# Feed-forward of a hybrid layer: a new block's token splits one product later and behind the emptying of banks; last product, sum and statistics in column halves

## The chip, the cores and the metric

The kernel runs on one core of a Trainium2 chip. The metric is the device time of one execution in microseconds (us), lower is better. Engines are named as in the profile: PE (TensorE, matmuls), PEld (its weight loads), DVE (VectorE), ACT (ScalarE), POOL (GpSimd), SP (SyncE, which here issues DMAs). Each runs its own instructions in their order and waits for the others by semaphores. PSUM, where PE writes its results, is used in banks of 512 float32 columns.

## The reference, cut to what matters

One layer over 2048 prompt tokens and 8 x 16 sample tokens, with D_MODEL = 1024 and D_FF = 2816. The first part (mLSTM heads, sliding-window attention, output projection, layer norm) isn't touched. The change lies in the feed-forward part and the norm behind it:

```python
def conv_ffn(h, conv_prev, w_up, w_conv, b_conv, w_down):
    T = h.shape[1]
    u = h @ w_up
    ext = jnp.concatenate([conv_prev.astype(u.dtype), u], axis=1)
    c = b_conv + sum(ext[:, j:j + T] * w_conv[j] for j in range(CONV_W))
    a, g = jnp.split(c, 2, axis=-1)
    return (jax.nn.silu(g) * a) @ w_down, ext[:, -(CONV_W - 1):]
...
    f, conv_rows = conv_ffn(h, conv_prev, w_up, w_conv, b_conv, w_down)
    y = layer_norm(DEEPNORM_ALPHA * h + f, ln2_g, ln2_b)
```

All values are float32.

## The kernel before

**Tiles and blocks.** The 17 tiles of 128 tokens are taken in three blocks (`FBLOCKS`): tiles 0 to 5, 6 to 11, and 12 to 16, the last with the sample tokens. The up projection goes, for each block b, over 22 pairs j of column groups (128 value columns and the 128 gate columns that belong to them). Each pair is computed by seven products s = 1 to 7 in the manner of Strassen, from sums of weights and sums of tokens. `f_product` (L1889) issues a product: 12 matmuls, whose moving operand has half the block's tokens as its columns, 384 for blocks 0 and 1 and 320 for block 2. Float32 precision comes from splitting each operand into a high part (ACT casts it, L220) and the low rest (DVE subtracts, L221) in `split`: weights into `uw`, tokens into `hh` (high) and `hl` (low), in the down projection tokens into `fu`.

**Order of the products.** PE's order is that in which the code is written. `self.seq` gives the products of pair j as 6, 2, 5, 3, 4, where the next pair's product 1 stands between 5 and 3, and its product 7 between 3 and 4. A pair holds three PSUM banks A, B, C, in the pool `fup` for even j and `dps` for odd j. Products 1 and 2 go to A, 6, 5 and 3 to B, 7 and 4 to C, and they add up in place, so a bank has to be emptied between certain products.

**Emptying banks.** `f_after` (L1899) does that behind each product: after 1 a copy of A to B (ACT L1910); after 6 a copy of B to `u2` (ACT L1925); after 2 A to `u` (ACT L1927); after 5 B to `u4` (ACT L1929), then C + `u4` to `u` (DVE L1930, and L1932 for the sample tokens); after 3 B to `u` (ACT L1934, L1936); after 4 C + `u2` to `u` (DVE L1939), and then the convolution on `cc` (ACT L1943, DVE L1945) and in `f_gate` the gate `th` (ACT L1967, DVE L1968, L1969), which SP stores to `zf`.

**Tokens of the next block.** At the last pair of a block (j = 21), `f_tokens` (L1764) makes a new block's operands step by step: product s of the old block is followed by the cast and subtraction for the new block's product s, and by sums of tokens in place, `t1` to `t4` (DVE, `hraw`, L1773, L1775, L1777, L1779).

**Order of the other engines.** ACT, DVE, POOL and SP get their order from a scheduler that looks at what each instruction needs and how long it takes in a model of its own. `issue_after(ins)` makes the instructions of a code section that go to the engine of `ins` stand behind `ins` on that engine.

**Down projection.** `f_downs` (L2065) does seven products again per block, each in six units of two tiles of its inner dimension. `d_weights` (wraw to `uw`) and `d_tokens` (r, loaded from `zf`, to `fu`) split its operands ahead of time; the first of them are called in `f_ups` at the last pair of the last block. Results are added to `yacc` (DVE L2128), and normed. The last product of the kernel is s = 3 of block 2, column groups p = 2, 1, 0 in that order; `norm_last` (L1576) takes statistics (BN_STATS, aggregation), and writes the tile out.

Of the kernel before, what the change touches and what calls it, by code (L numbers as in the profile page):

```python
# [14 lines left out]
P = 128  # L15
# [31 lines left out]
HT = 2 * P  # L47
# [157 lines left out]
class Prog:  # L205
# [1380 lines left out]
    def stats(self, y, st=None):  # L1586
        nc = self.nc
        V = nc.vector
        half = st is not None
        if not half:  # L1590
            st = self.wp.tile([P, 2, 6], F32, name="lst", tag="lst", bufs=2)
        mv = self.wp.tile([P, 2], F32, name="lmv", tag="lmv", bufs=2)
        s = self.wp.tile([P, 2], F32, name="lsc", tag="lsc", bufs=2)
        for i in range(half, 2):
            V.bn_stats(st[:, i], y[:, i * 512:(i + 1) * 512])
        V.bn_aggr(mv, st)
# [242 lines left out]
    def f_ups(self, n):  # L1839
        nc = self.nc  # L1840
        for _ in range(AHEAD - n):
            self.f_next()

        self.banks = [[pool.tile([P, 512], F32, name=n, tag=n) for _ in range(3)] for pool, n in ((self.fup, "fup"), (self.dps, "dps"))]
        self.f_written(0)
        self.f_tokens(0, 2)
        late = self.o_late()
        nb = len(FBLOCKS)
        nxt = None
        for i, (b, j, s) in enumerate(self.seq):  # L1850
            if s == 6 and j == 6 and b + 1 < nb:
                nxt = self.f_hT(b + 1)
            if i == 4:
                self.f_written(1)
            if (b, j, s) == (nb - 2, NFF // 2, 6):
                hist = self.f3.tile([P, 2, 2, NFF, DB, 2], F32, name="hist", tag="hist", bufs=1)
                self.sconv, self.convs = hist[:, 0], hist[:, 1]
                nc.sync.dma_start(self.sconv, self.a["sconv"].rearrange("p (v j) b r -> p v j b r", v=2))
            self.f_product(b, j, s)
            while self.made < min(i + 1 + (AHEAD if b == 0 else AHEAD + 2), len(self.seq)):  # L1860
                self.f_next()
            self.f_after(b, j, s)
            if i < 4:
                self.f_tokens(0, *((5,), (3,), ("t4",), (4,))[i])
            if j >= 2 and s in (6, 5):
                next(late, None)
            if nxt and s in (6, 5):
                next(nxt, None)
            if b + 1 < nb and j == NFF - 1:
                if s == 1:  # L1870
                    for _ in nxt:
                        pass
                    nxt = None
                self.f_tokens(b + 1, *{1: (1, "t1", "t3"), 7: (7, "t2"), 6: (6,), 2: (2,), 5: (5, "t4"), 3: (3,), 4: (4,)}[s])
            if b == nb - 1 and j == NFF - 3 and s == 6:
                self.d_begin()
            if b == nb - 1 and j == NFF - 1 and s not in (1, 7):
                self.d_weights()
                if s != 4:
                    self.d_tokens()  # L1880
        nc.sync.dma_start(self.a["conv_p"], self.prev.rearrange("p v j r -> p (v j) r"))
        nc.sync.dma_start(self.a["conv_s"], self.convs.rearrange("p v j b r -> p (v j) b r"))

    def f_written(self, i):

# [13 lines left out]
    def f_after(self, b, j, s):  # L1899
# [6 lines left out]
        WP = W - P if has_s else W  # L1906
        n = WP + (DB * (DS + 2) if has_s else 0)
        A, B, C = [x[:, :h] for x in self.banks[j % 2]]
        if s == 1:
            S.copy(B, A)  # L1910
            return
        if s == 7:
            return
# [8 lines left out]
        m = WP - h  # L1922
        dec = lambda z: z[:, m:].rearrange("p (b l) -> p b l", b=DB)
        if s == 6:
            S.copy(u2, B)  # L1925
        elif s == 2:
            S.copy(u[:, 0, 2:2 + h], A)  # L1927
        elif s == 5:
            S.copy(u4, B)  # L1929
            V.tensor_add(u[:, 1, 2 + h:2 + WP], C[:, :m], u4[:, :m])  # L1930
            if has_s:
                V.tensor_add(us[:, 1, :, 2:], dec(C), dec(u4))  # L1932
        elif s == 3:
            S.copy(u[:, 0, 2 + h:2 + WP], B[:, :m])  # L1934
            if has_s:
                S.copy(us[:, 0, :, 2:], dec(B))  # L1936
        if s != 4:
            return
        V.tensor_add(u[:, 1, 2:2 + h], C, u2)  # L1939
# [125 lines left out]
    def f_downs(self):  # L2065
# [22 lines left out]
        nb, nu = len(FBLOCKS), len(DUNITS)  # L2088
        ys, ops = {}, {}
        last_tile = FBLOCKS[-1][0]  # L2090
        st = self.wp.tile([P, 2, 6], F32, name="st", tag="st", bufs=1)

        def product(s, p, units):
            ps = banks[role[s][2 if p == np_ else p]]
            c = slice(p * P, p * P + P)
            for u in units:
                wh, wl, fh, fl = ops[u]
                n = len(DUNITS[u])
                for k in range(n):
                    for i, (l, r) in enumerate(((fh, wh), (fh, wl), (fl, wh))):  # L2100
                        mm(ps, l[:, k, c], r[:, k], start=s in (1, 4, 7) and u == 0 and k == 0 and i == 0,  # L2101
                           stop=u == nu - 1 and k == n - 1 and i == 2, skip_group_check=True)
# [37 lines left out]
        for g, (b, s, u) in enumerate(self.dseq):  # L2140
# [52 lines left out]
```

## Time and profile before

| | |
|---|---|
| median of 3 runs | 2309.79 us (2309.2 to 2310.85) |
| the profiled execution | 2309.77 us |
| its span on the core | 2308.0 us |
| mean granted clock of PE | 0.998 |
| PE busy | 2275.2 us (99%), 14425 matmuls |
| DVE busy | 1806.0 us (78%), 3157 instructions |
| ACT busy | 1305.2 us (57%), 2465 instructions |
| POOL busy | 228.0 us (10%) |

The span is the time between the first and the last record on the core. Rows of a timeline give start, duration, engine, line, operation, `written tile <- read tiles`, shape and count; in brackets stand the idle time of that engine ahead of the row and what ended it. In timelines a tile's name is that of the program; `u` also stands for `u2` and `u4`. Line numbers are those of the kernel before. Up to 1249 us the up projection is in block 0, from there to 1577 in block 1, then to 1848 in block 2; the down projection follows.

### The profile page before, as it was taken

What the parts mean: (1) busy time and instruction counts of PE and PEld (TensorE: products, weight loads), DVE (VectorE), ACT (ScalarE), POOL (GpSimd) and SP (SyncE); (2) the same over time, 40 slices, a digit from 0 to 9 for tenths busy, and PEclk for the clock granted to TensorE, in tenths of its full rate; (3) what the DMA queues carried; (4) which work ended last, traced back from release to release, by engine and by line L of the source; (5) the groups of instructions that cost most, each with busy time, mean ns of one, the idle gap of its engine ahead of it and who ended that gap; (6) DMA issues with size and microseconds to landing.
All of it is one profiled execution on the core that took longest, in us unless ns stands there. A gap on an engine that the chain in (4) does not pass through costs nothing.

```text
span 2308.0 us, 39905 instructions
## 1 busy us (share of the span) xinstructions
PE 2275.2 (99%) x14425; PEld 2096.7 (91%) x14425; DVE 1806.0 (78%) x3157; ACT 1305.2 (57%) x2465; POOL 228.0 (10%) x289
## 2 busy tenths in 40 slices
PE   8999999999999999999999999999999999999998
PEld 8999999999877778999999999999999988888887
DVE  8777687786689888987888667778766787796897
ACT  5453466776766565555556455556555544654753
POOL 0001001001122121200002000002000000000100
PEclk9999999999999999999999999999999999999999
DMA  8898998889976667787777899888998786756753
GB/s 276 303 316 288 303 321 313 296 301 330 303 253 220 225 209 254 274 323 281 279 270 258 281 310 322 307 305 269 333 293 261 241 286 224 241 196 224 242 188 110
DMA packets 297365, 624.98 MB, mean 271 GB/s; under 512 B 47052, under 2 KB 140240, under 8 KB 297168
## 3 DMA queue, kind: packets, MB, share of 16 engines
q1 hardware_dynamic: 296304, 619.29, 78.4%
q10 hardware_dynamic: 864, 3.15, 0.4%
q8 instruction: 114, 1.87, 0.3%
q14 instruction: 83, 0.68, 0.1%
HBM read 451.78 MB, written 170.56 MB: 270 GB/s over the span
## 4 chain that ended last, share of the span: by engine, by line
PE 71%; DVE 7%; issue 3%; ACT 2%; DMA 2%; POOL 1%; SPq 0%; DVEq 0%; POOLq 0%; ACTq 0%
PE dps L1897 19%; PE fup L1897 19%; PE dps L2101 6%; PE fht L2101 6%; PE fup L2101 5%; PE dps L750 5%; PE dps L225 2%; PE dps L227 2%; PE dps L226 2%; PE ppo L1386 1%; DVE w L221 1%; PE psc L1337 1%; PE ppt L1380 1%; PE dps L775 1%; DMA txy<-wdn 1%
## 5 line engine op out<-in xcount | busy, mean ns | idle before, releaser
L1897 PE MATMUL dps<-hh,uw 128*128 128x384 f32 (+1 forms) x1848 | 477.4, 327 | 5.3 <-DVE u L1930 2.6
L1897 PE MATMUL fup<-hh,uw 128*128 128x384 f32 (+1 forms) x1848 | 476.4, 326 | 0.0
L1945 DVE SCALAR_TENSOR_TENSOR cc<-u,cw,cc 128x768 f32<-128x768 f32 (+1 forms) x264 | 257.8, 978 | 124.4 <-ACT cc L1943 121.0
L1897 PEld LDWEIGHTS dps<-hh,uw 128*128 128x128 f32 x1848 | 329.2, 188 | 7.6 <-DVE u L1930 3.2
L1897 PEld LDWEIGHTS fup<-hh,uw 128*128 128x128 f32 x1848 | 329.3, 188 | 0.0
L1897 PE MATMUL fup<-hl,uw 128*128 128x384 f32 (+1 forms) x924 | 301.3, 326 | 1.5 <-DVE hl L221 1.5
L1897 PE MATMUL dps<-hl,uw 128*128 128x384 f32 (+1 forms) x924 | 301.0, 326 | 0.0
L750 PE MATMUL dps<-w,oh 128*128 128x256 f32 x1344 | 250.5, 282 | 3.5 <-DMA w<-zws 1.8
L750 PEld LDWEIGHTS dps<-w,oh 128*128 128x128 f32 x1344 | 209.3, 188 | 15.8 <-issue 9.6
L220 ACT CAST uw<-wraw 128x1024 fp32r<-128x1024 f32 x126 | 123.3, 981 | 173.7 <-PE dps L2101 104.2
L221 DVE TENSOR_TENSOR w<-wraw,w 128x1024 fp32r<-128x1024 f32 (+1 forms) x155 | 180.9, 1172 | 47.5 <-ACT w L220 45.4
L220 ACT CAST w<-wraw 128x1024 fp32r<-128x1024 f32 (+1 forms) x155 | 155.3, 1009 | 95.7 <-PE dps L750 44.6
L221 DVE TENSOR_TENSOR uw<-wraw,uw 128x1024 fp32r<-128x1024 f32 x126 | 142.6, 1132 | 64.0 <-ACT uw L220 63.8
L750 PE MATMUL dps<-w,ol 128*128 128x256 f32 x672 | 186.2, 277 | 0.0
L1943 ACT ACTIVATE cc<-u,cw 128x768 f32<-128x768 f32 (+1 forms) x132 | 131.9, 1000 | 94.9 <-DVE u L1939 92.1
L1897 PEld LDWEIGHTS fup<-hl,uw 128*128 128x128 f32 x924 | 173.5, 188 | 2.4 <-DVE hl L221 2.4
L1897 PEld LDWEIGHTS dps<-hl,uw 128*128 128x128 f32 x924 | 173.5, 188 | 0.0
L750 PE MATMUL dps<-oh,w 128*128 128x256 f32 x896 | 167.2, 282 | 4.8 <-ACT zev L808 1.6
L2101 PE MATMUL fup<-uw,fu 128*128 128x512 f32 x726 | 169.0, 389 | 0.0
L2101 PEld LDWEIGHTS fup<-uw,fu 128*128 128x128 f32 x726 | 136.2, 188 | 28.2
L2101 PE MATMUL dps<-uw,fu 128*128 128x512 f32 x660 | 161.0, 389 | 0.1
L750 PEld LDWEIGHTS dps<-oh,w 128*128 128x128 f32 x896 | 139.7, 188 | 11.3 <-issue 4.1
(346 smaller groups left out, 4599.4 us busy)
## 6 DMA issues: line engine op xcount, KB each, us to landing
uw<-zw SPq DMA_DIRECT2D x176, 512.0 KB, 4.9
zw<-uw SPq DMA_DIRECT2D x88, 512.0 KB, 3.0
w<-zws SPq DMA_DIRECT2D x72, 512.0 KB, 6.3
wv<-wup SPq DMA_DIRECT2D x66, 512.0 KB, 5.8
wraw<-wi SPq DMA_DIRECT2D x62, 512.0 KB, 5.2
wraw<-zt SPq DMA_DIRECT2D x60, 512.0 KB, 4.3
wraw<-wdn SPq DMA_DIRECT2D x45, 512.0 KB, 3.8
wraw<-wo SPq DMA_DIRECT2D x40, 512.0 KB, 4.8
```

Source lines behind the costliest of these rows:

```text
L220: nc.scalar.copy(hi, src)
L221: nc.vector.tensor_sub(lo, src, hi.bitcast(F32))
L225: mm(out, ah, bh, start=start, stop=False)
L226: mm(out, ah, bl, start=False, stop=False)
L227: mm(out, al, bh, start=False, stop=stop)
L750: mm(o, l, r, start=s in (1, 7) and c == k == i == 0, stop=k == 3 and i == 2, skip_group_check=True)
L775: mm(o, x, w, start=k == i == 0, stop=k == KD - 1 and i == 2, skip_group_check=True)
L1337: nc.tensor.matmul(ps[kvh][:, j, :nk], q[rs, j0 + j], k[rs, sel], start=i == 0, stop=i == 2)
L1897: mm(ps, l[:, k], r[:, k], start=s in (1, 7) and k == 0 and i == 0, stop=k == 3 and i == 2, skip_group_check=True)
L1943: S.activation(c[:, v], u[:, v, 2:2 + n], AF.Identity, bias=w[3], scale=w[2])
L1945: V.scalar_tensor_tensor(c[:, v], u[:, v, i:i + n], w[i], c[:, v], op0=ALU.mult, op1=ALU.add)
L2101: mm(ps, l[:, k, c], r[:, k], start=s in (1, 4, 7) and u == 0 and k == 0 and i == 0, stop=u == nu - 1 and k == n - 1 and i == 2, skip_grou ...
```

## The change

There are three edits.

1. At the last pair of a block, the step of `f_tokens` that belonged behind product s is put into a list `put` and done after the next product. It is issued within `self.behind()`, which puts every instruction in it behind the instructions that empty the banks of that next product, on the engine of each: `f_after` now collects them in `self.gone`.
2. At the last pair of the last block, `d_weights` and `d_tokens` are issued within `self.behind()` too, at the same product as before.
3. The last product's last column group (p = 0) is done in two halves of 256 columns, 27 matmuls each, both in the one bank that it had. Each half is followed by its own addition (`scalar_tensor_tensor`) and statistics (`bn_stats`), so that the statistics tile has 4 groups in place of 2. The statistics behind product 2 of the same tile are taken in two pieces too. The two halves read the same weights, so PE has 54 matmuls of 256 columns for 27 of 512.

```diff
@@ stats @@
-        for i in range(half, 2):
+        for i in range(half if not half or st.shape[1] == 2 else 2, 2):
             V.bn_stats(st[:, i], y[:, i * 512:(i + 1) * 512])
@@ f_ups @@
-                self.f_tokens(b + 1, *{1: (1, "t1", "t3"), 7: (7, "t2"), 6: (6,), 2: (2,), 5: (5, "t4"), 3: (3,), 4: (4,)}[s])
+                put.append((i, b + 1, {1: (1, "t1", "t3"), 7: (7, "t2"), 6: (6,), 2: (2,), 5: (5, "t4"), 3: (3,), 4: (4,)}[s]))
+            if put and put[0][0] < i:
+                _, to, steps = put.pop(0)
+                with self.behind():
+                    self.f_tokens(to, *steps)
             if b == nb - 1 and j == NFF - 3 and s == 6:
                 self.d_begin()
             if b == nb - 1 and j == NFF - 1 and s not in (1, 7):
-                self.d_weights()
-                if s != 4:
-                    self.d_tokens()
+                with self.behind():
+                    self.d_weights()
+                    if s != 4:
+                        self.d_tokens()
+    def behind(self):
+        es = ExitStack()
+        for i in self.gone:
+            es.enter_context(self.tc.issue_after(i.ins))
+        return es
@@ f_after @@
+        self.gone = []
+        gone = self.gone.append
...
-            S.copy(u4, B)
-            V.tensor_add(u[:, 1, 2 + h:2 + WP], C[:, :m], u4[:, :m])
+            gone(S.copy(u4, B))
+            gone(V.tensor_add(u[:, 1, 2 + h:2 + WP], C[:, :m], u4[:, :m]))
...
@@ f_downs @@
-        st = self.wp.tile([P, 2, 6], F32, name="st", tag="st", bufs=1)
+        st = self.wp.tile([P, 4, 6], F32, name="st", tag="st", bufs=1)
-        def product(s, p, units):
-            ps = banks[role[s][2 if p == np_ else p]]
+        def product(s, p, units, q=slice(0, 512)):
+            ps = banks[role[s][2 if p == np_ else p]][:, q]
...
-                        mm(ps, l[:, k, c], r[:, k], start=s in (1, 4, 7) and u == 0 and k == 0 and i == 0,
+                        mm(ps, l[:, k, c], r[:, k, q], start=s in (1, 4, 7) and u == 0 and k == 0 and i == 0,
...
-                    V.bn_stats(st[:, 0], ys[ta][:, :512])
+                    for i in range(2):
+                        V.bn_stats(st[:, i], ys[ta][:, i * HT:i * HT + HT])
...
-                self.norm_last(ys[t], *ln2, a["y"][t], st if t == last_tile else None)
+                self.norm_last(ys[t], *ln2, a["y"][t], None)
...
-                for p in cols:
+                for p in cols[:-1]:
                     product(s, p, range(1, nu))
                     after(s, p)
                     for _ in pending.pop():
                         pass
+                y = ys[last_tile]
+                for i in range(2):
+                    q = slice(i * HT, i * HT + HT)
+                    product(s, cols[-1], range(1, nu), q)
+                    z = y[:, 512:][:, q]
+                    V.scalar_tensor_tensor(z, z, ALPHA, banks[role[s][cols[-1]]][:, q], op0=ALU.mult, op1=ALU.add)
+                    V.bn_stats(st[:, 2 + i], z)
+                self.norm_last(y, *ln2, a["y"][last_tile], st)
```

The scheduler's order on DVE, ACT and SP changes at the three places where a block ends; PE's is the same but for the last product. In the new file the lines of `f_after` and `f_gate` stand 14 further down (L1930 is L1944, L1939 is L1953, L1945 is L1959), but L1910 is L1924.

DVE at the end of block 0, from the first split of the new block's tokens, before:

```order
L221 TENSOR_TENSOR hl_15202<-hraw,hh_15201 128x1536
L221 TENSOR_TENSOR uw<-wg,uw 128x512
L1773 TENSOR_TENSOR hraw<-hraw 128x4x384
L1945 TENSOR_SCALAR cc<-u,cw,cc 128x768
L1775 TENSOR_TENSOR hraw<-hraw 128x4x384
L1939 TENSOR_TENSOR u<-fup,u_15142 128x384
L1945 TENSOR_SCALAR cc<-u,cw,cc 128x768
L221 TENSOR_TENSOR uw<-wv,uw 128x512
L221 TENSOR_TENSOR hl_15240<-hraw,hh_15239 128x1536
L1945 TENSOR_SCALAR cc<-u,cw,cc 128x768
L1777 TENSOR_TENSOR hraw<-hraw 128x4x384
L1945 TENSOR_SCALAR cc<-u,cw,cc 128x768
```

And now:

```order
L221 TENSOR_TENSOR uw<-wg,uw 128x512
L221 TENSOR_TENSOR hl_15218<-hraw,hh_15217 128x1536
L1959 TENSOR_SCALAR cc<-u,cw,cc 128x768
L1773 TENSOR_TENSOR hraw<-hraw 128x4x384
L1953 TENSOR_TENSOR u<-fup,u_15142 128x384
L1775 TENSOR_TENSOR hraw<-hraw 128x4x384
L1959 TENSOR_SCALAR cc<-u,cw,cc 128x768 x2
L221 TENSOR_TENSOR hl_15264<-hraw,hh_15263 128x1536
L1959 TENSOR_SCALAR cc<-u,cw,cc 128x768
L1777 TENSOR_TENSOR hraw<-hraw 128x4x384
L221 TENSOR_TENSOR uw<-wv,uw 128x512
L1944 TENSOR_TENSOR u<-dps,u_15285 128x384
```

The first `hl` has gone behind the weight split `uw<-wg`, and the add from the bank C (`u<-dps`, L1930, now L1944) has come forward: before, it stood behind two more `hl`, which follow it now.

ACT at the end of block 2, from the copy to `u2` of product 6 (L1925, now L1939) to the copy to `u4` of product 5 (L1929, now L1943), before:

```order
L1925 COPY u_21339<-dps 128x320
L220 COPY fu<-r_21083 128x768
L220 COPY fu<-r_21083 128x384
L1927 COPY u<-dps 128x320
L220 COPY uw<-wraw 128x1024
L1967 ACTIVATE th<-cc 128x656
L1929 COPY u_21340<-dps 128x320
```

And now, from the cast ahead of it:

```order
L220 COPY fu<-r_21083 128x384
L1939 COPY u_21339<-dps 128x320
L220 COPY uw<-wraw 128x1024
L220 COPY fu<-r_21083 128x768
L1981 ACTIVATE th<-cc 128x656
L1941 COPY u<-dps 128x320
L220 COPY uw<-wraw 128x1024
L220 COPY fu<-r_21083 128x768
L1943 COPY u_21340<-dps 128x320
```

Casts for the down projection (`uw<-wraw`, `fu<-r`) that stood ahead of the `u2` copy stand behind it now, so two `uw` and two `fu` of 768 columns lie between the two copies where one `uw` and two `fu` lay.

DVE at the same place, to the add of product 4 (L1939, now L1953), before:

```order
L1968 TENSOR_SCALAR th<-th,cc 128x656
L1930 TENSOR_TENSOR u<-dps,u_21340 128x192
L1969 TENSOR_TENSOR th<-th,cc 128x656
L1932 TENSOR_TENSOR u<-dps,u_21340 128x8x16
L221 TENSOR_TENSOR uw<-wraw,uw 128x1024
L221 TENSOR_TENSOR fu<-r_21083,fu 128x768
L1939 TENSOR_TENSOR u<-dps,u_21339 128x320
```

And now:

```order
L221 TENSOR_TENSOR uw<-wraw,uw 128x1024
L221 TENSOR_TENSOR fu<-r_21083,fu 128x768
L1982 TENSOR_SCALAR th<-th,cc 128x656
L221 TENSOR_TENSOR uw<-wraw,uw 128x1024
L1983 TENSOR_TENSOR th<-th,cc 128x656
L221 TENSOR_TENSOR fu<-r_21083,fu 128x768
L1944 TENSOR_TENSOR u<-dps,u_21340 128x192
L1946 TENSOR_TENSOR u<-dps,u_21340 128x8x16
L221 TENSOR_TENSOR uw<-wraw,uw 128x1024
L221 TENSOR_TENSOR fu<-r_21083,fu 128x768
L221 TENSOR_TENSOR uw<-wraw,uw 128x1024
L221 TENSOR_TENSOR fu<-r_21083,fu 128x768
```

The add of product 4 follows as the next row: two `uw` and two `fu` stand between it and the adds of product 5, where one pair stood.

PE at the kernel's end, with the waits that an instruction carries, now:

```order
L2115 MATMUL dps<-uw,fu 128x512 [waits DVE_49]
L2115 MATMUL dps<-uw,fu 128x512
L2115 MATMUL fht<-uw,fu 128x512 x27
L2115 MATMUL fht<-uw,fu 128x256 x27
L2115 MATMUL fht<-uw,fu 128x256 [waits DVE_49]
L2115 MATMUL fht<-uw,fu 128x256 x26
```

Before, the last column groups were 54 matmuls of 512 columns without a wait among them; now the second half's first matmul waits for an instruction of DVE, which is the first half's addition from the same bank.

More of the change, by code (lines that the diff above doesn't have):

```diff
@@ L1847, in f_ups @@
         late = self.o_late()
-        nb = len(FBLOCKS)
+        nb, put = len(FBLOCKS), []
         nxt = None
@@ L1908, in f_after @@
         A, B, C = [x[:, :h] for x in self.banks[j % 2]]
+        self.gone = []
+        gone = self.gone.append
         if s == 1:
-            S.copy(B, A)
+            gone(S.copy(B, A))
             return
@@ L1924, in f_after @@
         if s == 6:
-            S.copy(u2, B)
+            gone(S.copy(u2, B))
         elif s == 2:
-            S.copy(u[:, 0, 2:2 + h], A)
+            gone(S.copy(u[:, 0, 2:2 + h], A))
         elif s == 5:
-            S.copy(u4, B)
-            V.tensor_add(u[:, 1, 2 + h:2 + WP], C[:, :m], u4[:, :m])
+            gone(S.copy(u4, B))
+            gone(V.tensor_add(u[:, 1, 2 + h:2 + WP], C[:, :m], u4[:, :m]))
             if has_s:
-                V.tensor_add(us[:, 1, :, 2:], dec(C), dec(u4))
+                gone(V.tensor_add(us[:, 1, :, 2:], dec(C), dec(u4)))
         elif s == 3:
-            S.copy(u[:, 0, 2 + h:2 + WP], B[:, :m])
+            gone(S.copy(u[:, 0, 2 + h:2 + WP], B[:, :m]))
             if has_s:
-                S.copy(us[:, 0, :, 2:], dec(B))
+                gone(S.copy(us[:, 0, :, 2:], dec(B)))
         if s != 4:
             return
-        V.tensor_add(u[:, 1, 2:2 + h], C, u2)
+        gone(V.tensor_add(u[:, 1, 2:2 + h], C, u2))
         c = self.f3.tile([P, 2, 768], F32, name="cc", tag="cc", bufs=2)[:, :, :n]
```

## The prediction, made before the changed kernel was run

> **What bounds the kernel now.** I read the page's busy times first: PE is busy 99% of the span of 2308.0 us, so the edits can matter only where PE waits, or after its last product. I went through PE's timeline at the two block changes, at the change to the down projection and at the end, then the chain of waits and the other engines there. PE's stops, in start, duration, engine, line, operation and idle time with its releaser:
>
> ```profile
> 1249.60 0.34 PE L1897 MATMUL fup<-hh,uw 128*128 128x384 f32 x1
> 1250.82 0.44 PE L1897 MATMUL dps<-hh,uw 128*128 128x384 f32 x1 [0.88 <-DVE u L1930]
> ...
> 1575.05 0.31 PE L1897 MATMUL fup<-hh,uw 128*128 128x320 f32 x1
> 1577.08 0.45 PE L1897 MATMUL dps<-hh,uw 128*128 128x384 f32 x1 [1.73 <-DVE u L1930]
> ...
> 1843.12 0.31 PE L1897 MATMUL dps<-hh,uw 128*128 128x320 f32 x1
> 1844.53 0.42 PE L1897 MATMUL dps<-hh,uw 128*128 128x320 f32 x1 [1.10 <-ACT u L1929]
> ```
>
> Records of queued matmuls overlap, so I count from start to start. A 384-column matmul starts 0.17 us after the one before it (6.24 us for 36), a 320-column one 0.15 (5.27 for 36): a product of 12 takes 2.08 or 1.76. PE thus loses 1.05, 1.88 and 1.26 us at these seams; each time product s=4 or 3 wants a bank that DVE or ACT has not emptied. All three seams together hold 4.2 us.
>
> ```profile
> 1548.86 6.24 PE fup L1897 x36
> 1579.43 5.27 PE fup L1897 x36
> ```
>
> **Seam from block 0 to 1.** ACT's and DVE's timelines:
>
> ```profile
> 1231.63 1.48 ACT L220 CAST hh<-hraw 128x1536 fp32r<-128x1536 f32 x1
> 1233.53 0.47 ACT L1934 COPY u<-fup 128x384 f32<-128x384 f32 x1
> ...
> 1233.14 1.76 DVE L221 TENSOR_TENSOR hl<-hraw,hh 128x1536 fp32r<-128x1536 f32 x1 [1.82 <-ACT hh L220]
> 1237.09 1.01 DVE L1945 SCALAR_TENSOR_TENSOR cc<-u,cw,cc 128x768 f32<-128x768 f32 x1
> 1246.88 3.42 DVE L221 TENSOR_TENSOR hl<-hraw,hh 128x1536 fp32r<-128x1536 f32 x2
> 1250.22 0.55 DVE L1930 TENSOR_TENSOR u<-dps,u 128x384 f32<-128x384 f32 x1
> ```
>
> DVE stands idle 1.82 us ahead of the first hl and then never until the add on which PE waits. Queued operations overlap by about 0.08 (two hl in 3.34, where one is 1.75), so a place in this queue costs hl or hraw 1.67, cc 0.93, u 0.47 and uw (0.69 for 512, below) 0.60. After the change the cast of hh sits behind ACT's copy of product 3, so it cannot begin before that copy has run: hh lands about 1233.7 and hl begins about 1235.25 (the copy's own start is PE-bound, about 1233.3, since the cast ahead of it is gone). The uw split of 0.60 that followed hl runs in the gap. DVE therefore has 2.1 - 0.6 = 1.5 us less of its queue done when hl starts. The add L1930 goes forward past several splits, which clears the old stall, but those splits are still due. In the new order DVE has from hl up to the add that empties C for the next column pair's product 4: 7 hl and 4 hraw (11 x 1.67), 8 cc (7.44), 4 u (1.88) and 5 uw (3.0), 30.7 us, all queued. That add starts at 1235.25 + 30.7 - 0.47 = 1265.5, and PE restarts 0.60 after an add's start (1250.82 against 1250.22), at 1266.1. Unstalled, PE wants that bank seven products after 1249.77, at 1264.33. So it loses 1.75 in place of 1.05: **+0.7**. Bounds: 0, if DVE has hidden slack, and +1.5, the lost DVE time in full.
>
> **Seam from block 1 to 2.** The same edit, with 320 columns:
>
> ```profile
> 1559.30 0.48 ACT L1934 COPY u<-fup 128x384 f32<-128x384 f32 x1
> 1558.89 1.49 DVE L221 TENSOR_TENSOR hl<-hraw,hh 128x1280 fp32r<-128x1280 f32 x1 [1.24 <-ACT hh L220]
> 1575.00 0.95 DVE L1969 TENSOR_TENSOR th<-th,cc 128x768 f32<-128x768 f32 x1
> 1576.47 0.55 DVE L1930 TENSOR_TENSOR u<-dps,u 128x384 f32<-128x384 f32 x1
> ```
>
> hl moves from 1558.89 to about 1560.98 (copy to 1559.7, cast 1.27). Up to the add stand 6 hl or hraw at 1.40, 4 cc, u, 2 th (1.8) and 2 uw, 15.6, then the add itself: it ends at 1577.1, where it ended before at 1577.02. Nothing is won here, because the splits that went behind it only paid for the lateness. They now come after it: 4 hl, 1 hraw (7.0), 4 cc (3.7), 3 uw (1.8), and the adds of both products (0.95), 13.5 more, to 1590.6. PE wants that bank after one product of 2.08 and six of 1.76, 12.64 after its restart at 1577.2, at 1589.8. A new stop of 0.8 to 1.05: **+1.0**, bounds 0 and +1.5.
>
> **Seam into the down projection.** ACT first, then DVE:
>
> ```profile
> 1837.55 0.84 ACT L220 CAST fu<-r 128x768 fp32r<-128x768 f32 x1
> 1840.07 0.41 ACT L1925 COPY u<-dps 128x320 f32<-128x320 f32 x1
> 1842.08 1.05 ACT L220 CAST uw<-wraw 128x1024 fp32r<-128x1024 f32 x1
> 1843.41 0.75 ACT L1967 ACTIVATE th<-cc 128x656 f32<-128x656 f32 x1 [0.27 <-DVE cc L1945]
> 1844.07 0.41 ACT L1929 COPY u<-dps 128x320 f32<-128x320 f32 x1
> ...
> 1846.17 1.22 DVE L221 TENSOR_TENSOR uw<-wraw,uw 128x1024 fp32r<-128x1024 f32 x1
> 1847.30 0.95 DVE L221 TENSOR_TENSOR fu<-r,fu 128x768 fp32r<-128x768 f32 x1
> 1848.43 0.49 DVE L1939 TENSOR_TENSOR u<-dps,u 128x320 f32<-128x320 f32 x1 [0.18 <-PE dps L1897]
> 1852.49 0.55 DVE L221 TENSOR_TENSOR fu<-r,fu 128x384 fp32r<-128x384 f32 x1
> 1854.67 0.84 DVE L1968 SCALAR_TENSOR_TENSOR th<-th,cc 128x656 f32<-128x656 f32 x1 [0.82 <-ACT th L1967]
> 1855.43 0.69 DVE L221 TENSOR_TENSOR uw<-wraw,uw 128x512 fp32r<-128x512 f32 x1
> ```
>
> Before, ACT had cast early what it now keeps for later. From the u2 copy (begun 1840.25, after a small fu cast) to the u4 copy it now has uw, fu, th, a u copy, uw and fu between the two copies; at the rows' durations less some 0.1 of overlap 0.96 + 0.73 + 0.66 + 0.32 + 0.96 + 0.73 = 4.36. With 0.32 for the u2 copy and 0.41 for u4 that ends about 1845.35. PE is ready at 1843.27, so it stops 2.1 in place of 1.26: +0.8. Next late is DVE: from the first uw (about 1841.9) it has uw, fu, th, uw, th, fu (1.14 + 0.87 + 0.76 + 1.14 + 0.76 + 0.87) and the two u adds, to about 1848.0, while PE wants bank C at 1845.45 + 1.76 = 1847.2: a second stop, between 0.3 and 0.9, 0.8 by the longer durations that follow a cross-engine wait. Together **+1.55**.
>
> Then the last gate. Behind the second u add DVE has uw, fu, uw, fu (4.0) before it adds product 4, so the add starts at 1851.9 where it started at 1848.43: 3.5 late. The fu after it grows from 384 to 768 columns (+0.4), a uw slips into the idle 0.82 (-0.6). The last th is 3.3 to 3.4 late, of which 1.55 is PE's own delay: 1.75 is new. Who waits: SP stores th to zf, reads it back as r, and DVE, ACT and PE follow. The chain of waits runs through it until PE:
>
> ```profile
> 1857.28 4.09 DMA zf<-th
> ...
> 1895.33 2.79 PE dps L2101 x11
> ```
>
> As this chain had no slack before, the lateness arrives in full at 1895: **+1.75**; bounds 0, if the loads are held by something else, and 2.5, if they queue behind shifted loads.
>
> **Costed at nothing.** SP's loads at the seams move by a place or two; PE's releasers there are DVE and ACT, so the loads have been early, and if one is not, it lies within the bounds above. The statistics of product 2's half in two pieces (one more DVE operation, under 0.5) run under the PE work ahead of the last product. No instruction of POOL changes its place.
>
> **Tail.** PE, DVE, and last a row of 256-column matmuls from earlier in the kernel:
>
> ```profile
> 2288.01 12.40 PE L2101 MATMUL fht<-uw,fu 128*128 128x512 f32 x54
> 2294.33 0.69 DVE L2128 SCALAR_TENSOR_TENSOR yacc<-yacc,fht 128x512 f32<-128x512 f32 x1 [0.72 <-PE fht L2101]
> 2297.41 1.41 DVE L1583 SCALAR_TENSOR_TENSOR yacc<-yacc,lsc,f_ln_b 128x512 f32<-128x512 f32 x2
> 2300.45 0.69 DVE L2128 SCALAR_TENSOR_TENSOR yacc<-yacc,fht 128x512 f32<-128x512 f32 x1 [1.63 <-PE fht L2101]
> 2301.89 0.21 DVE L1596 BATCH_NORM_AGGREGATE lmv<-st 128x2 f32<-128x12 f32 x1
> ...
> 77.14 1.60 PE L759 MATMUL psx<-w,xs 128*128 128x256 f32 x12
> ```
>
> 54 matmuls of 512 come at 0.227; 27 end about 2294.15. A 256-column one is near 0.116 (11 starts in 1.32), so halving costs nothing by itself: the first half is done by 2297.4. Both halves share one bank, and in the new order the second half's first matmul waits on DVE, on the first half's add. That add is queued behind the norm of the tile before, to 2298.75, and takes some 0.42, an estimate along the line from 0.69 for 512 columns and 0.49 for 320. PE restarts at 2299.2, needs 27 x 0.116 = 3.1 to 2302.35, and after it come 0.15 of drain, add and statistics of 256, near 0.45 each: aggregation at 2303.5 in place of 2301.89, **+1.65**. Without the wait it would be PE at 2300.4 and aggregation at 2301.3, -0.55: these are the bounds.
>
> The Trainium skill ("PSUM — Partial Sum Buffer", section "PSUM bank collisions raise a hardware error") says to guard PSUM by bank and quadrant, not by address, since two engines collide at different addresses of one bank too. By that rule the halves of one bank cannot overlap, which is the +1.65; by addresses alone it would be the -0.55. No run here shows a collision.
>
> **Sum.** 0.7 + 1.0 + 1.55 + 1.75 + 1.65 = 6.65. The profiled execution took 2309.77, beside the median of 2309.79, so 2316.5.
>
> **Rivals.** *The seams clear* (other side): PE's three stops of 4.2 go and the tail overlaps (-0.55), 2305.0. It decides if DVE has 2 us of spare time within the 17 us after a block change, or the second half needs no add. For it: the adds on which PE waits do move forward. Against: DVE's only idle there lies ahead of hl, and it grows. 6%. *The lateness is absorbed* at the two block changes and in the down chain, leaving 1.55 + 1.65: 2313.0. For it: DVE later idles again (78% busy); against: PE needs the bank within 15 us. 17%. *The down chain drags more*: the later splits free wraw and r later, and one more transfer like zf<-th, 4.09 from issue to landing, comes to lie on the path for some 2.5 of it: 2319. 9%. *The clock drops* at the tail's stop of 1.7 us, and the last 27 matmuls take twice their 3.1: 2319.6, 2%. Against it stands a stop of 1.88 us, after which this row grants 1.00 (its last three columns are clock, DMA share, GB/s):
>
> ```profile
> 1576.80:1590.00 13.20, 12.92 (x86) 12.92 (x87) 12.92 (x16) 6.94 (x13) 5.56 (x4) 1.00 0.68 221
> ```
>
> The Trainium skill ("TensorE: Matmul & The Clock Gate", section "Part 1: The HAM clock gate") puts the drop after an idle window of about 3.4 us; the trace agrees as far as it goes, with 1.88 us and no drop.
>
> **How the numbers follow.** My forecast has 66%: 2316.5. Its terms' bounds give 2311.5 with the chains slack and 2319 with them long; that takes in the absorbed case and leaves out the cleared seams and the far ends. This kernel's measurement tells about 0.2%, 4.6 us, from no change. Faster: 6%. Same: absorbed 15 and the forecast's low edge 4, 19%. Slower: 62 of the forecast, 11 of the last two, 2 of the absorbed, 75%.
>
> **What would show it.** At both block changes: DVE's idle ahead of the first hl near 3.3 and 2.7 in place of 1.82 and 1.24, no PE stop at block 0's last product 4, one of about 1.5 fifteen microseconds later; two stops of 1.9 and 1.0 after block 1. Into the down projection two stops, 2.1 and 0.8, and the last th 3.3 late against its place before. At the end a hole of some 1.7 us in the middle of the last product's 54 short matmuls. No hole, or PE stops shorter than before, would make it wrong.

## The result, and the profile after

The changed kernel takes 2326.1 us (median of 6 runs, 2324.34 to 2329.03) where the kernel before takes 2310.32 (6 runs, 2309.2 to 2313.08). The ratio is 1.0065, with a 95% interval of 1.0054 to 1.0075: 15 us slower, between 12.5 and 17.3. The forecast was 2316.5, in a range of 2311.5 to 2319. The direction was right; the time lies outside the range, and some 8 to 10 of the 15 us have another cause than any that was named.

The profiled execution has a span of 2324.7 us (2308.0 before) and a granted clock of 0.999. PE's busy time is the first thing to look at. It was 2275.2 us and is now this:

```profile
PE 2292.4 (99%) x14452; PEld 2111.7 (91%) x14452; DVE 1806.3 (78%) x3160; ACT 1305.3 (56%) x2465; POOL 216.1 (9%) x289
```

PE has 27 matmuls more, since 54 of half the width stand for 27, so its work is the same. Yet it is *busy* 17 us longer; stops would show as idle time instead. PE's stops in the timeline after (start, duration, engine, line, operation, idle time with its releaser) are these:

```profile
1260.08 0.44 PE L1909 MATMUL fup<-hl,uw 128*128 128x384 f32 x1 [0.19 <-DVE hl L221]
1273.81 0.44 PE L1909 MATMUL fup<-hh,uw 128*128 128x384 f32 x1 [1.14 <-DVE u L1944]
...
1586.94 0.45 PE L1909 MATMUL dps<-hh,uw 128*128 128x384 f32 x1 [1.80 <-DVE u L1944]
1600.41 0.41 PE L1909 MATMUL fup<-hh,uw 128*128 128x320 f32 x1 [0.52 <-DVE u L1946]
...
1855.82 0.41 PE L1909 MATMUL dps<-hh,uw 128*128 128x320 f32 x1 [1.91 <-ACT u L1943]
1858.38 0.41 PE L1909 MATMUL dps<-hh,uw 128*128 128x320 f32 x1 [0.54 <-DVE u L1946]
...
2314.08 3.49 PE L2115 MATMUL fht<-uw,fu 128*128 128x256 f32 x27 [1.70 <-DVE yacc L2187]
```

They stand where the prediction put them: the old stop at the change to block 1 is gone and one of 1.14 follows 13.7 us later, the other two changes have two stops each, and there is a hole in the middle of the last product. They don't make 15 us.

PE's order is the same in both kernels up to the last product, so the n-th matmul of one trace is that of the other. How late the changed kernel starts the same matmul shows the stages:

```
matmul, and when it starts before            later in the change by   in this stage
 6789,  916 us  start of the up projection        6.1                    6.1
 8700, 1249 us  last pair of block 0              7.7                    1.6
 9000, 1302 us  past the change to block 1        8.6                    0.9
10550, 1568 us  last pair of block 1              9.8                    1.2
10700, 1593 us  past the change to block 2       10.7                    0.9
12380, 1839 us  last pair of block 2             10.5                   -0.2
12470, 1855 us  past the change to down          12.2                    1.7
12643, 1895 us  where the old chain ended        12.5                    0.3
14370, 2288 us  last column groups               14.8                    2.4
the span's end                                   16.7                    1.9
```

Six microseconds are lost before the feed-forward begins, in code that the change doesn't touch and whose instructions stand in the same order. The view of groups by shape shows how (line, engine, operation, count, busy us, mean ns of one, idle time before). First the kernel before, then the change:

```profile
L750 PE MATMUL dps<-w,oh 128*128 128x256 f32 x1344 | 250.5, 282 | 3.5 <-DMA w<-zws 1.8 <-DVE zev L822 0.8 <-ACT zev L808 0.6
L750 PE MATMUL dps<-w,ol 128*128 128x256 f32 x672 | 186.2, 277 | 0.0
L750 PE MATMUL dps<-oh,w 128*128 128x256 f32 x896 | 167.2, 282 | 4.8 <-ACT zev L808 1.6 <-DVE zev L820 1.2 <-ACT oh L544 1.1
L1897 PE MATMUL fup<-hl,uw 128*128 128x384 f32 x616 | 206.1, 335 | 1.5 <-DVE hl L221 1.5
L2101 PE MATMUL fup<-uw,fu 128*128 128x512 f32 x726 | 169.0, 389 | 0.0
L1897 PE MATMUL fup<-hh,uw 128*128 128x320 f32 x616 | 144.4, 309 | 0.0
```

```profile
L750 PE MATMUL dps<-w,oh 128*128 128x256 f32 x1344 | 256.5, 285 | 1.7 <-DMA w<-zws 0.6 <-ACT zev L808 0.6 <-DVE zev L822 0.4
L750 PE MATMUL dps<-w,ol 128*128 128x256 f32 x672 | 188.2, 280 | 0.0
L750 PE MATMUL dps<-oh,w 128*128 128x256 f32 x896 | 171.7, 285 | 4.5 <-ACT zev L808 1.5 <-ACT oh L544 1.2 <-DVE zev L820 0.9
L1909 PE MATMUL fup<-hl,uw 128*128 128x384 f32 x616 | 207.4, 337 | 1.8 <-DVE hl L221 1.8
L2115 PE MATMUL fup<-uw,fu 128*128 128x512 f32 x726 | 170.3, 391 | 0.0
L1909 PE MATMUL fup<-hh,uw 128*128 128x320 f32 x616 | 144.4, 309 | 0.5 <-DVE u L1946 0.5
```

The matmuls of 256 columns from `w` and `oh` or `ol` are 3 ns longer on average, those of 384 and 512 are 2 ns, those of 320 are not. A few nanoseconds are nothing on one instruction, but line L750 has 3360 of them, so 3 ns make some 10 us. Part of that falls into waits that PE had there anyway (in the first row its idle time shrinks from 3.5 to 1.7), and 6 us are left. What the first 900 us share with the change is memory: a tile's place is fixed for the whole program. The statistics tile `st` grew from 2 x 6 to 4 x 6 floats, 48 to 96 bytes per partition, which take 64 and 96 in the compiled program's table of tiles. What is placed behind it lies 32 bytes further, among it `oh`, `ol`, part of `hh` and `hl`, `r`, `u`, `cc`, `yacc`, and two of the ten slots of `uw`. The `w` of L750 and the `fu` stay where they were. The theory for the experiments is that this shift slows the matmuls that read there; its rivals are the placement of the instructions, and the waits.

### The profile page after: what moved, and what is told of

It is laid out like the page before. It is cut to its first block, busy times and chain, and to the rows that moved or that the text cites. A ratio compares the mean times of both kernels' runs of the same rounds, so it can differ in the third digit from the quotient of the medians.

```text
span 2324.7 us, 39954 instructions
## 1 busy us (share of the span) xinstructions
PE 2292.4 (99%) x14452; PEld 2111.7 (91%) x14452; DVE 1806.3 (78%) x3160; ACT 1305.3 (56%) x2465; POOL 216.1 (9%) x289
## 4 chain that ended last, share of the span: by engine, by line
PE 85%; DVE 9%; issue 3%; DMA 2%; ACT 1%; SPq 0%; POOL 0%; DVEq 0%; ACTq 0%; POOLq 0%
PE fup L1909 19%; PE dps L1909 18%; PE dps L750 15%; PE fup L2115 6%; PE dps L2115 6%; PE fht L2115 5%; PE dps L225 2%; PE dps L775 2%; PE dps L227 2%; PE dps L226 1%; PE ppo L1386 1%; PE psc L1337 1%; DVE w L221 1%; DVE uw L221 1%; PE ppt L1380 1%
## 5 line engine op out<-in xcount | busy, mean ns | idle before, releaser
L1959 DVE SCALAR_TENSOR_TENSOR cc<-u,cw,cc 128x768 f32<-128x768 f32 (+1 forms) x264 | 257.6, 978 | 128.8 <-ACT cc L1957 125.6
L750 PE MATMUL dps<-w,oh 128*128 128x256 f32 x1344 | 256.5, 285 | 1.7 <-DMA w<-zws 0.6
L750 PEld LDWEIGHTS dps<-w,oh 128*128 128x128 f32 x1344 | 211.1, 188 | 13.4 <-issue 8.9
L750 PE MATMUL dps<-w,ol 128*128 128x256 f32 x672 | 188.2, 280 | 0.0
L750 PE MATMUL dps<-oh,w 128*128 128x256 f32 x896 | 171.7, 285 | 4.5 <-ACT zev L808 1.5
L750 PEld LDWEIGHTS dps<-oh,w 128*128 128x128 f32 x896 | 141.1, 188 | 11.1 <-issue 4.1
```

The costliest lines, as they stand in the source:

```text
L750: mm(o, l, r, start=s in (1, 7) and c == k == i == 0, stop=k == 3 and i == 2, skip_group_check=True)
L1959: V.scalar_tensor_tensor(c[:, v], u[:, v, i:i + n], w[i], c[:, v], op0=ALU.mult, op1=ALU.add)
```

## The experiments

A lateness is that of PE against the kernel before at the same matmul, in one profile of each. At 916 us kernels that are alike up to there differ from -1.3 to +3.4 us in single profiles (in the two with the most the clock had fallen at 893 us, see the last section), so lateness is read by stage behind that point, and the pace of equal matmuls ahead of it. The medians of the kernel before, taken anew beside each group of runs, lie between 2309.69 and 2310.4.

**The statistics tile alone.** Only the size is changed; no instruction moves.

```diff
-        st = self.wp.tile([P, 2, 6], F32, name="st", tag="st", bufs=1)
+        st = self.wp.tile([P, 4, 6], F32, name="st", tag="st", bufs=1)[:, :2]
```

> The kernel before, with only the statistics tile st made [P, 4, 6] as in the change and two of its four groups used: 96 bytes per partition for 48, every instruction in its old order, tiles allocated behind st (oh, ol, part of hh and hl, r, u, cc, yacc and two of ten uw slots) 32 bytes further. Theory 'addresses' (the pace of matmuls in the changed kernel falls because operands start 32 bytes off a 64-byte boundary): slower by 10 to 12 us, some 2320.5 to 2322, with PE about 6 us late at the start of the up projection and 9 to 9.5 us late at the end of its block 1, and no new stop at a seam. Rival 'instructions' (more and differently placed instructions slow PE): 2310, no difference. Rival 'seams' (all the rest comes from the new waits): 2310.

Measured: 2319.99, ratio 1.0036 (1.0023 to 1.0049), about 8 us slower, just less than was expected. The lateness is 6.0 us at 916 us, 7.5 at the last pair of block 1, where 9 or more was expected, and 10.8 at the last column groups. The changes between blocks have no new stop; there is one of 0.6 in block 2, at 1680.6. The 256-column group has the changed kernel's mean:

```profile
L750 PE MATMUL dps<-w,oh 128*128 128x256 f32 x1344 | 256.5, 285 | 0.9 <-DMA w<-zws 0.7 <-ACT zev L816 0.2
```

The instructions are those of the kernel before in the same order with the same waits, so neither a new instruction nor a new wait did it. The matmuls of `psx<-w,xs` serve as a control: they have 256 columns too, neither of their operands moved, and they keep their pace (117.6 ns from start to start on average, before and here).

**The whole change at the old addresses.** The four statistics groups live in a spacer that the down projection has anyway, and a spacer of 64 bytes holds the place of `st`.

```diff
-        self.skew(self.fp, 480)
+        st = self.fp.tile([P, 120], F32, name="skew", tag="skew480", bufs=1)[:, :24].rearrange("p (i k) -> p i k", k=6)
...
-        st = self.wp.tile([P, 4, 6], F32, name="st", tag="st", bufs=1)
+        self.skew(self.wp, 64)
```

> The changed kernel whole, but with the four statistics groups kept in a spacer of 480 bytes that the down projection has anyway, and a spacer of 64 bytes in the place of st: all tiles at the addresses of the kernel before, all instructions in the order of the change. Theory 'addresses': pace as before, the new stops stay: 0.6 + 0.8 + 1.6 at the seams and 1.7 to 2 at the end, 2310 + 5 = 2314 to 2316. Rivals 'instructions' and 'seams': 2325 to 2327, as the change.

Measured: 2315.71, ratio 1.0022 (1.0013 to 1.0031), 5 us slower, as expected. The two halves, 1.0036 and 1.0022, make 1.0058 together where the change has 1.0065, within their intervals. The lateness at 916 us is -0.5 now, and the 256-column group of `w` and `oh` is back at 283 ns.

**Which way, and how far.** Six more sizes and places. `st` of 120 bytes moves the same tiles by 64:

> The kernel before with the statistics tile of 120 bytes, which takes 128: the same tiles as in the run with 96 bytes now 64 bytes further, not 32. Theory 'addresses' in the form 'off a 64-byte boundary': 2310, no difference. In the form 'any move hurts, since the spacers were chosen for these very addresses': 2315 to 2322. Rivals: 2310.

Measured: 2324.77, ratio 1.0057 (1.0044 to 1.0069): worse than by 32 (its fastest execution is slower than the slowest of that run), and above the 2322 expected. A 64-byte boundary is not the rule. Only the first part's tiles by 32 further, and by 32 nearer (`skew(self.xp, 288)` and `skew(wx, 416)`, then 224 and 480, for 256 and 448):

> The kernel before with the 32 bytes put only under the tiles of the first part (oh, ol and its working tiles), and taken back ahead of the feed-forward's. Theory 'addresses': the share of the first 880 us alone, +5 to +6 us, 2315 to 2316, with matmuls of 256 columns from oh and ol going from 0.114 to 0.117 us, and the feed-forward at its old pace. Rivals: 2310.

> The kernel before with the tiles of the first part 32 bytes nearer to the start, the feed-forward's at their old place. If the pace goes by the distance from the old address in the same direction as the steps seen (0.114 us as before, 0.118 with 32 more, 0.120 with 64 more): 0.111 and 6 us faster in the first 880 us, 2304. If the old address is the best one or the two sides are alike: 0.117 and 2314 to 2316.

Measured: 2314.62, ratio 1.0017 (1.0008 to 1.0027), with 117 to 118 ns from start to start, by the medians, where `oh` and `ol` took 113 to 114, and no lateness added behind 916 us; and 2317.15, ratio 1.0027 (1.0017 to 1.0038), with 117 to 118 ns too. Both sides of the old address are slower, so the hoped-for gain of 6 us isn't there. Only the feed-forward's tiles by 32 (`skew(self.wx, 736)` for 704):

> The kernel before with 32 bytes more only ahead of the feed-forward's tiles; the first part at its old addresses. If the shares add up: nothing up to 915 us, +2 to +3 in the up projection's blocks 0 and 1, next to nothing in block 2 (320 columns), +2.5 to +3 in the down projection, 2314.5 to 2316 in all; the rival that the loss is one thing of the whole program and not of the operands: 2310 or 2320.

Measured: 2315.69, ratio 1.0026 (1.0017 to 1.0036). Behind 916 us the lateness grows by 0.2 in block 0 and the change to block 1, by 1.2 in block 1, not at all in block 2, and by 2.8 in the down projection. By the medians the two shares, 4.2 and 5.4 us, add up to the 9.6 that the shift of all tiles costs (by the ratios, some 4 and 6 where it costs 8, which their intervals allow). Last, all tiles by 128 and by 256:

> The kernel before with st taking 192 bytes for 64: the same tiles 128 bytes further. 32 less, 32 more and 64 more have all been slower. If the pace comes back with a period of 128 bytes: 2310. If the period is longer: 2320 to 2326.

> The same with 320 bytes, tiles 256 bytes further. If the pace comes back with a period of 256 bytes or less: 2310. If the period is 512 or more, or it is no matter of a period: 2318 to 2328.

Measured: 2324.43, ratio 1.0065 (1.0049 to 1.008); and 2308.44, ratio 0.9997 (0.9988 to 1.0006). With 256 bytes the pace is back, in every group:

```profile
L750 PE MATMUL dps<-w,oh 128*128 128x256 f32 x1344 | 250.6, 282 | 2.1 <-DVE zev L822 1.1 <-DMA w<-zws 0.6 <-ACT zev L816 0.3
L2101 PE MATMUL fup<-uw,fu 128*128 128x512 f32 x726 | 169.0, 389 | 0.0
```

In the down projection the moving operand is `uw`, the stationary one `fu`, which never moved. Only two of the ten `uw` slots did, the high and low part of every fifth unit. Start-to-start times there in ns, means of six matmuls in a row, from matmul 13100 on, in the kernel before, in the changed kernel (32 bytes on) and with 256 bytes:

```
before        226.7 226.7 226.7 226.7 226.7 226.7 226.7 226.7 226.7 226.7 226.7 226.7 226.7 226.7 226.7 226.7 226.7 226.7 226.7 226.7 226.7 226.7
32 bytes on   226.7 226.7 226.7 226.7 228.2 233.3 231.7 230.2 226.7 226.7 226.7 226.7 226.7 226.7 226.7 226.7 226.7 226.7 231.7 233.2 233.5 232.0
256 bytes on  226.7 226.7 226.7 226.7 226.7 226.7 226.7 226.7 226.7 226.7 226.7 226.7 226.7 226.7 226.7 226.7 226.7 226.7 226.7 226.7 226.7 226.7
```

One unit in five takes up to 233 ns for 227, as one unit in five has its moving operand in a shifted slot; the others keep their time to a tenth of a nanosecond. So the loss goes with the operand's place, matmul by matmul, and not with a load on the memory as a whole.

**The first edit alone, at the old addresses.** The diff is the part of the change in `f_ups` on `f_tokens`, with `behind` and `gone`.

> The kernel before with the first edit alone (a new block's splits one product later and behind the emptying), all tiles at their old addresses. Theory 'DVE is late by the same work': +0.6 at the change to block 1 and +0.8 to +1.7 at the change to block 2, 2311.5 to 2312.5 in all, with a PE stop about 13 us after each change that was not there; the end as before. Rival 'the edit clears the stops and its loss in the changed kernel came from the slower matmuls': -2.9, 2307.

Measured: 2310.98, ratio 1.0004 (0.9995 to 1.0013), less than expected, and not to be told from no change; the stages can. The change to block 1 costs 0.7, that to block 2 costs 1.7, and the stop of 1.12 after the first is there as in the change:

```profile
1253.01 0.44 PE L1908 MATMUL fup<-hl,uw 128*128 128x384 f32 x1 [0.23 <-DVE hl L221]
1266.74 0.45 PE L1908 MATMUL fup<-hh,uw 128*128 128x384 f32 x1 [1.12 <-DVE u L1943]
...
1578.48 0.44 PE L1908 MATMUL dps<-hh,uw 128*128 128x384 f32 x1 [1.86 <-DVE u L1943]
```

The rival, that the stops clear, falls: without the slower matmuls they cost what they did with them, and at the change to block 2 more. The second stop after block 1 is missing here for another reason, told in the last section.

**One product later, but not behind the emptying.**

```diff
-                with self.behind():
-                    self.f_tokens(to, *steps)
+                self.f_tokens(to, *steps)
```

> The kernel before with the new block's splits one product later, but not put behind the emptying, at the old addresses. Theory 'DVE is late by the idle time ahead of the first hl': the first hl as early as before or near to it, the add that PE waits for ahead of two splits, and the stops at the two block changes shorter than before: -0.5 to -2, 2308 to 2309.5. Rival 'one product later is the loss': +1.3 to +2.5 as with the whole edit.

Measured: 2308.4, ratio 0.9995 (0.9986 to 1.0004). By stage it gains 0.8 at the change to block 1 and 0.6 at that to block 2. The first hl is as early as before, behind the same idle 1.82:

```profile
1231.49 1.76 DVE L221 TENSOR_TENSOR hl<-hraw,hh 128x1536 fp32r<-128x1536 f32 x1 [1.82 <-ACT hh L220]
```

In the change that idle time is 0.99 and 2.25 around one weight split:

```profile
1239.91 0.69 DVE L221 TENSOR_TENSOR uw<-wg,uw 128x512 fp32r<-128x512 f32 x1 [0.99 <-ACT uw L220]
1242.85 1.76 DVE L221 TENSOR_TENSOR hl<-hraw,hh 128x1536 fp32r<-128x1536 f32 x1 [2.25 <-ACT hh L220]
```

So the first edit has a half that gains 1.4 us by the stages, which two medians can't tell from nothing, and a half that loses more: `issue_after` on the copy makes DVE wait.

**The second edit alone, at the old addresses.** `d_weights` and `d_tokens` within `self.behind()`.

> The kernel before with the second edit alone (the down projection's first splits behind the emptying), at the old addresses. Theory: two stops of 2.1 and 0.7 at the change to the down projection in place of one of 1.26, +1.5 to +1.7, and nothing at 1895 us, since the chain from th by zf to r has slack: 2311.5 to 2312. Rival, as the prediction had it: the last th 3.3 late and the chain without slack, +3.3, 2313.

Measured: 2310.37, ratio 1.0004 (0.9995 to 1.0014), again less than expected. The lateness rises by 2.3 at the change to the down projection (0.7 more than in the change itself, for which the last section has a fall of the clock) and by 0.06 from there to matmul 12643 at 1895 us. The prediction's last gate costs nothing.

**The last product's halves in two banks, at the old addresses.** What the old bank held is added ahead of the last two column groups; the halves of the rest start in two banks that are free by then.

```diff
+                add(last_tile, 1, banks[role[s][cols[-1]]], True)
...
-                    product(s, cols[-1], range(1, nu), q)
+                    product(s, cols[-1], range(1, nu), q, banks[i][:, :HT])
-                    V.scalar_tensor_tensor(z, z, ALPHA, banks[role[s][cols[-1]]][:, q], op0=ALU.mult, op1=ALU.add)
+                    V.tensor_add(z, z, banks[i][:, :HT])
```

> The kernel before with the third edit, but with the halves in two banks that are free by then (what the old bank held is added to yacc ahead of the last two column groups), at the old addresses. Theory 'the shared bank costs the end': no hole in the 54 short matmuls, aggregation 0.5 earlier than before against 1.8 later in the change, 2309.5 to 2310 beside 2310. Rival 'the halves themselves cost' (54 short matmuls slower than 27 long ones, or DVE held by the norm of the tile ahead): +0.5 or more.

Measured: 2309.22, ratio 0.9995 (0.9986 to 1.0005). The hole is gone, in PE's and DVE's timelines at the end:

```profile
2295.23 6.63 PE L2101 MATMUL fup<-uw,fu 128*128 128x256 f32 x54
...
2299.85 0.41 DVE L2174 TENSOR_TENSOR yacc<-yacc,fup 128x256 f32<-128x256 f32 x1
2301.90 0.42 DVE L2174 TENSOR_TENSOR yacc<-yacc,fup 128x256 f32<-128x256 f32 x1 [1.18 <-PE fup L2101]
2302.82 0.26 DVE L1596 BATCH_NORM_AGGREGATE lmv<-skew 128x2 f32<-128x24 f32 x1
```

PE is 1.1 us late here by its first part, so aggregation is at 2301.7 in the kernel before's time, for 2301.89: a gain of 0.2, where 0.5 was expected. The 54 short matmuls take 6.63 us from the first start to the last end where 27 long ones took 6.28, and that is the rest. In the change the same rows stand 2 us further apart:

```profile
2313.62 0.41 DVE L2187 SCALAR_TENSOR_TENSOR yacc<-yacc,fht 128x256 f32<-128x256 f32 x1
2317.61 0.42 DVE L2187 SCALAR_TENSOR_TENSOR yacc<-yacc,fht 128x256 f32<-128x256 f32 x1 [3.12 <-PE fht L2115]
2318.52 0.26 DVE L1596 BATCH_NORM_AGGREGATE lmv<-st 128x2 f32<-128x24 f32 x1
```

## Why the prediction was wrong

**The step that failed** is the one under "costed at nothing": the statistics in smaller pieces were counted as one more DVE operation of under 0.5 us, hidden under PE. The tile that holds them was not looked at. Its growth from 48 to 96 bytes moves every tile placed behind it, and that costs 8 us by the run with the tile alone, about 11 of its profile's span, where the whole change has 15 and 16.7. The prediction held each matmul's duration for given and asked only for waits; 3 ns on a 256-column matmul was outside all of its rivals. One other step failed, the last gate below. Where the prediction looked at stops, its signs came: DVE idle for 3.24 us ahead of the first hl (3.3 was named), the pairs of stops, and a hole of 1.70 in the last product.

**The change to block 1**: +0.7 predicted, +0.7 measured in the run with the first edit alone; the change has 0.9, of which the run with the tile alone has 0.1 too. Stops of 0.34 and 1.31, counted from start to start, stand for one of 1.05. The old stop goes, and DVE's lateness comes due 13.7 us later, as the sum over its queue said. Its start held too: hl begins at 1242.85, which is 1235.2 without the lateness of 7.7, where 1235.25 was said. (The 1233.7 at which hh was said to land is where its cast begins.)

**The change to block 2**: +1.0 predicted, +0.9 measured. The stop that stays is 1.97 against 1.88, the new one 0.69.

**The change to the down projection**: +1.55 predicted, +1.6 measured (1.7 less 0.1 of pace), by stops of 2.07 and 0.70 where the prediction had 2.1 and 0.8.

**The last gate**: +1.75 predicted, nothing measured, in the change and in the run with the second edit alone. The last th starts at 1869.68, 13.6 later than before (1856.03), of which 10.5 is PE's lateness up to this seam: 3.1, near the 3.3 predicted. But the step "as this chain had no slack before" was wrong. The trace of before had a row that says so:

```profile
1876.69 0.84 ACT L220 CAST fu<-r 128x768 fp32r<-128x768 f32 x1 [1.46 <-PE fup L2101]
```

Here, between the loads of r and the matmul at 1895 at which the chain reached PE, ACT waits 1.46 us for PE to free a `fu` buffer, so the data of r were there already. DVE's sums, on which that matmul hangs, follow this cast (1878.55 before, 1890.91 after, 12.4 apart where PE is 12.2 late). The chain of waits had stepped from r's load to a load of yacc and from there to DVE: it names the event that came last, not one that DVE needed.

**The tail**: +1.65 predicted, +1.8 measured (2318.52 less a lateness of 14.8, against 2301.89), and shown by the run with two banks to be the wait on the shared bank. By the Trainium skill's rule ("PSUM — Partial Sum Buffer", section "PSUM bank collisions raise a hardware error") a bank is one thing to be guarded; the trace agrees in that the second half's first matmul stood 1.70 us for an addition of other columns.

The five terms measure 5.0 where 6.65 was predicted, and the change at the old addresses is 5 us slower (3.0 to 7.2): the forecast was a fair one for the kernel without the shift. That interval holds 6.65 as well, so it is the stages and not the times that show the last gate to cost nothing. The rival of cleared stops has fallen; that of a dragging down chain too.

## What to carry to other kernels

A tile's size is part of a change's cost even when nobody waits for the tile: list which tiles get another address, and compare the pace of equal matmuls in stages that the change doesn't touch before looking at any wait. When PE's busy time grows and its work doesn't, look at its pace. An order that puts work behind another engine's copy helps the waiter only if it doesn't stretch the idle time at the head of the queue; and before a chain is called tight, look for a wait on the bounding engine further along it.

## What the runs showed of the hardware that was not expected

**Pace by address.** A matmul of 256 columns from the first part's tiles takes 113 to 114 ns from start to start at the old address, 117 to 118 with 32 less or more, 119 to 120 with 64 more, 117 to 118 with 128 more, and 113 to 114 with 256 more (medians of the four groups of L750). Of 512 columns it takes 227 at the old address and with 256 more, up to 233 with 32 or 128 more where its moving operand lies in a moved slot. Those of 320 columns don't react.

Which of a matmul's two operands moves doesn't decide. A row names the moving operand first, and `w` never moved: in `dps<-w,oh` the stationary operand `oh` moved, in `dps<-oh,w` the moving one, and both groups went from 282 to 285 ns. With 128 bytes, the 384-column matmuls of blocks 0 and 1, sorted by the addresses in the compiled program, take 173.8 ns where both operands or neither lie in moved slots, and 176.2 where one does; so there it is the distance between the two that counts. With 64 bytes that rule fails (175.3 where both or neither moved, 173.2 where only the moving one did). Why the pace goes by address stays open.

**The clock can drop behind a stop of 2 us.** In three runs at the old addresses PE stopped for 2.0 to 2.1 us, counted from start to start, and came back at half pace. The change at the old addresses, around its stop before 1576.2 (stretch, length, then busy time of PE, PEld, DVE, ACT and POOL, granted clock, DMA share, GB/s):

```profile
1573.80:1576.00 2.20, 0.53 (x4) 0.27 (x2) 2.20 (x3) 2.20 (x5) 0.00 (x0) 1.00 0.85 315
1576.00:1577.00 1.00, 0.81 (x4) 0.81 (x5) 1.00 (x2) 1.00 (x2) 0.73 (x1) 1.00 1.00 314
1577.00:1578.00 1.00, 1.00 (x5) 1.00 (x5) 1.00 (x2) 0.32 (x1) 0.59 (x1) 0.51 0.81 324
1578.00:1579.00 1.00, 1.00 (x5) 1.00 (x4) 1.00 (x2) 0.00 (x0) 0.00 (x0) 0.50 0.16 61
1579.00:1580.00 1.00, 1.00 (x5) 1.00 (x4) 1.00 (x1) 0.00 (x0) 0.00 (x0) 0.50 0.00 0
```

The clock falls to 0.50 about 0.8 us after the restart and stays there until about 1580.4. This seam costs 1.7 here where it costs 0.9 in the change: PE loses pace, and in return, it seems, comes late enough that its second stop for DVE is missing. Behind 1240 us four of five stops of 2.0 us or more ended so, two of them in this run, and none of the ten of some 1.9 at the change to block 2. The changed kernel itself stopped for 1.97 at the same place and for 2.07 at the next, and kept its clock; at the former:

```profile
1584.70:1586.80 2.10, 0.44 (x4) 0.18 (x2) 2.10 (x3) 2.10 (x4) 0.00 (x0) 1.00 0.92 343
1586.80:1588.00 1.20, 1.06 (x6) 1.06 (x7) 1.20 (x2) 1.20 (x2) 0.98 (x1) 1.00 1.01 264
```

The length of one stop isn't the whole rule. The kernel before has a drop itself, which the prediction didn't look at: PE stands idle for 2.68 us up to 155.6, and the granted clock is 0.50 from 156.4 to 159.8; 13 of the 14 profiles have this one. In two (the last product in two banks, and the feed-forward's tiles by 32) it fell at 893 us behind an idle time of only some 1.24, with shorter stops just ahead, while the run with the first edit alone kept its clock there behind the same 1.24. The prediction's argument against this rival, a stop of 1.88 without a drop, held for the change but is no rule. The Trainium skill ("TensorE: Matmul & The Clock Gate", section "Part 1: The HAM clock gate") asks for an idle window of about 3.4 us that runs freely; the traces agree that the same stop may or may not be hit, but show drops behind idle times of 1.24 to 2.68 us, shorter than the window.
